# Forget gate and key of eight recurrent heads from one Tanh in place of two Sigmoids

## Chip, cores and metric

The kernel runs on one core of a Trainium2 chip. The metric is the device time of one launch in microseconds (us). The profile gives one execution of the same program. Its engines are PE (matmul; PEld is the weight load that overlaps it), DVE (vector), ACT (scalar, activation functions), POOL (GpSimd) and SP, which issues most transfers. Each engine works through its own queue in order and waits on semaphores for the others.

## What is computed

The reference is one inference step of a one-layer streaming encoder with two parallel branches: an mLSTM with 4 heads of width 512, and an HGRN2 recurrence with 8 heads of width 128. It runs on 512 new frames and on 32 frames of a running stream; the kernel treats them side by side as 544 columns. The change lies in the gates of the HGRN2 branch, where every weight has `q_h`, `f_h`, `i_h`, `g_h` as slices of one projection:

```
lb = cumsum(softmax(hgrn_lb, axis=0))[0]      # one number per channel
lfh = log(lb + (1 - lb) * sigmoid(f_h))       # log of the forget gate
kh  = (1 - lb) * sigmoid(-f_h)                # key
qh  = silu(q_h)
oh, S_new = _hgrn(qh, kh, i_h, lfh, S0)       # linear recurrence with decay exp(lfh)
oh = head_rmsnorm(oh) * silu(g_h)
```

## The kernel before

Channels lie on the 128 partitions and the 544 time steps along the row. The program has four stretches: the input norm with the first projections and the convolution; four mLSTM heads; eight recurrent heads; and the merge of the branches with the output projections.

All large products are single-precision products from two halves: each weight piece is split into a high part (a copy on ACT, lines 191 and 204) and a low part (a subtraction on DVE, lines 196 and 205), and three matmuls stand for one. Pairs of projection units are multiplied with seven block products in place of eight (`class Two`), which needs sums of weight pieces on DVE (line 533, tiles `ws`). Their results are taken out of PSUM by ACT (line 592, tiles `t`) and DVE (lines 599 and 601), and the last block of a unit calls what is to be done with the finished tile.

In the stretch of the recurrent heads (lines 1630 to 2000) three things are woven together. `Pump` walks through the block products of the projections still to be made, PE instruction by PE instruction, in units of half a block of 12 matmuls (line 575). `chain(h)` makes head h's matrix of attention and decay in seven levels (1, 2, 4, ... 64 columns): per level four or more matmuls of 128x128 (line 1815, tile `pl`), which read keys copied by ACT into one shared buffer (`keys`, line 1770, tile `kmos`) and the decayed query and key (tile `hkq`, a pair `kk` and `qq`); then DVE multiplies both by the decays of the level (line 1836), POOL multiplies the decays pairwise (line 1843), and DVE puts the products under masks (lines 1850 to 1852). `tail(h)` makes states and outputs of the head before. In this stretch the order on ACT, DVE and PE is that in which the code issues instructions; the constants `STEPS`, `PDGAP`, `PIECES`, `FDELAY`, `QDELAY` say after how many half blocks each piece is issued.

When the unit `f` of a head is finished, `forget(h, t)` is called with the pre-activation in `t` (tile `tf`; the last part comes by ACT, line 603). It issues on ACT: a Sigmoid of -t into `kk` at once (line 1642), and by `pump.defer` a Sigmoid of t in place after 2 half blocks (1643), the scaling of `kk` by `lc` = 1 - lb after 2 (1644), and lb + lc * t in place after 5 (1645). When unit `q` is finished, `query(h, t)` issues a Silu of t (line 1650, tile `hq`) and, after 2 half blocks, the product of query and forget gate on DVE (line 1653), which writes `qq`. The matmuls of level 1 (line 1815) read `qq` and the copied keys; the product with no decay (line 1790, tile `pd`) reads `kk` and `hq`. Between two heads' `forget` and `query` stand weight copies, PSUM copies and key copies of other work.

The instruction that loads a function table into ACT (ACT_TABLE_LOAD) isn't in the code; it is put ahead of an activation whose function isn't in the loaded table, and has that activation's line.

`hgrn_bounds` (line 1401) makes lb and lc once, from 128x8 numbers, in the first mLSTM head. The rest of that head's order on ACT and DVE is set by a scheduler, not by hand.

Of the kernel before, what the change touches and what calls it, by code (L numbers as in the profile page):

```python
# [9 lines left out]
F32 = mybir.dt.float32  # L10
# [3 lines left out]
AF = mybir.ActivationFunctionType  # L14
ALU = mybir.AluOpType

P = 128
# [4 lines left out]
T = NS + NP  # L22
# [5 lines left out]
HH = 8  # L28
# [17 lines left out]
VTGAP = ((2, 1, 1, 1, 1), (1, 1, 1, 1, 1), (1, 1, 1, 1, 1), (0, 2, 2, 1, 1))  # L46
GAPS = (20, 20, 20, 14)
APART = 10
FDELAY = (2, 2, 5)
QDELAY = 2  # L50
FACTORS = 0
HOLDS = (0, 1, 3)
# [31 lines left out]
def hybrid_step(ctx: ExitStack, tc: tile.TileContext, a, o):  # L84
    nc = tc.nc
    V, S, G, PE = nc.vector, nc.scalar, nc.gpsimd, nc.tensor

    cp = ctx.enter_context(tc.tile_pool(name="cp", bufs=1))
# [21 lines left out]
    def slot(name, dt=F32):  # L110
        return sp.tile([P, WP + P // 2], dt, tag="s", name=name)

    def eslot(name, dt=F32):

        return sp.tile([P, SLOT], dt, tag="e", name=name, bufs=NEVAC)

    def epair(name, dt=F32):

        return sp.tile([P, 2, SLOT], dt, tag="ee", name=name, bufs=2)

    def small(name, shape, dt=F32, bufs=2, tag=None):
        return tp.tile(shape, dt, tag=tag or name, name=name, bufs=bufs)
# [345 lines left out]
    def plain(t):  # L468

        return t, tuple(((t[:, b * TH : (b + 1) * TH], slice(0, TH)),) for b in range(2))  # L470
# [189 lines left out]
    def pair(what, f, unit, dest, then):  # L660

        return Two(
            [((what, f + i), unit + i, lambda f=f + i: dest(f), lambda t, f=f + i: then(f, t)) for i in range(2)]
        )
# [158 lines left out]
    def fill(h):  # L823


        def value(f, t):
            st8[h]["vt"][f] = t

        def gate(f, t):
            act = S.activation(t[:, :T], t[:, :T], AF.Silu)  # L830
            st8[h]["z"][f] = (t, act)

        def gate_one(f, acc):
            z = eslot(f"z{h}{f}")
            for b in range(2):
                act = S.activation(z[:, b * TH : (b + 1) * TH], acc[b][:, :TH], AF.Silu)
            st8[h]["z"][f] = (z, act)

        def inner_tile(f):
            ub = conv_tile((h + 1) * KH + f)  # L840
            return ub, conv_parts(ub)

        def inner(f, ub):
            st8[h + 1]["ub"][f] = ub
            if f == 0:
                conv(h + 1)

        st8[h]["z"] = [None] * KH
        todo = []
        if h:  # L850
            st8[h]["vt"] = [None] * KH
            todo += [pair("v", f, 16 + h * KH + f, lambda f: plain(eslot(f"vt{h}{f}")), value) for f in (0, 2)]
            todo += [pair("z", f, 32 + h * KH + f, lambda f: plain(eslot(f"z{h}{f}")), gate) for f in (0, 2)]
        else:
            todo += [One(("z", f), 32 + f, TH, lambda acc, f=f: gate_one(f, acc)) for f in range(KH)]
        if h + 1 < MH:
            st8[h + 1]["ub"] = [None] * KH
            todo += [pair("u", f, (h + 1) * KH + f, inner_tile, inner) for f in (0, 2)]
        else:
            todo.append(next(hgrn))  # L860
        return todo
# [534 lines left out]
        st8[h].clear()  # L1396
        return made[f"wbm{h}31"][1]

    lb, lc = cp.tile([P, HH], F32, name="lb"), cp.tile([P, HH], F32, name="lc")

    def hgrn_bounds(decayed, masked):

        l0, l1 = vec[:, V_LB : V_LB + HH], vec[:, V_LB + HH : V_LB + 2 * HH]
        lm, le = small("lbm", [P, HH], bufs=1), small("lbe", [P, 2, HH], bufs=1)
        with tc.issue_after(masked.ins):
            V.tensor_tensor(lm, l0, l1, ALU.max)
            V.tensor_tensor(le[:, 0, :], l0, lm, ALU.subtract)
            V.tensor_tensor(le[:, 1, :], l1, lm, ALU.subtract)
        with tc.issue_after(decayed.ins):
            S.activation(le, le, AF.Exp)  # L1410

        def rest():
            V.tensor_tensor(lm, le[:, 0, :], le[:, 1, :], ALU.add)
            V.reciprocal(lm, lm)
            V.tensor_tensor(lb, le[:, 0, :], lm, ALU.mult)
            V.tensor_tensor(lc, le[:, 1, :], lm, ALU.mult)

        return rest

# [25 lines left out]
    with tc.manual_schedule(engines={mybir.EngineType.Activation, mybir.EngineType.DVE, mybir.EngineType.PE}):  # L1445
# [15 lines left out]
        for k in range(KD):  # L1461
            t = xt[k]
# [133 lines left out]
        pump = Pump(fill(0))  # L1596
# [38 lines left out]
    def units():  # L1635


        def forget(h, t):
            lbc, lcc = lb[:, h : h + 1], lc[:, h : h + 1]
            kq = epair(f"hkq{h}")  # L1640
            kk = kq[:, 0]
            S.activation(kk[:, :T], t[:, :T], AF.Sigmoid, scale=-1.0)
            pump.defer(FDELAY[0], lambda: S.activation(t[:, :T], t[:, :T], AF.Sigmoid))
            pump.defer(FDELAY[1], lambda: S.mul(kk[:, :T], kk[:, :T], lcc))
            pump.defer(FDELAY[2], lambda: S.activation(t[:, :T], t[:, :T], AF.Identity, scale=lcc, bias=lbc))
            hs[h].update(tf=t, kk=kk, kq=kq)

        def query(h, t):
            qq = hs[h]["kq"][:, 1]
            S.activation(t[:, :T], t[:, :T], AF.Silu)  # L1650
            hs[h].update(q0=t, qq=qq)
            tf = hs[h]["tf"]
            pump.defer(QDELAY, lambda: V.tensor_tensor(qq[:, :T], t[:, :T], tf[:, :T], ALU.mult))  # L1653

        def turned(t):

            return t, (
                ((t[:, HB - 1 : HB - 1 - TH : -1], slice(0, TH)),),
                ((t[:, HB - 1 - TH :: -1], slice(0, HB - TH)), (t[:, HB:T], slice(HB - TH, TH))),
            )  # L1660

        def value(h, t):
            hs[h]["ii"] = t

        def gate(h, t):
            S.activation(t[:, :T], t[:, :T], AF.Silu)
            hs[h]["gg"] = t

        def merge_a(f, t):
            S.activation(t[:, :T], t[:, :T], AF.Sigmoid)  # L1670
            y = slot(f"ya{f}")[:, :T]
            nc.sync.dma_start(y, ya_d[f])
            pump.defer(2, lambda: V.tensor_tensor(y, y, t[:, :T], ALU.mult))
            yas[f] = y

        def merge_b(f, t):
            S.activation(t[:, :T], t[:, :T], AF.Sigmoid)
            gbs[f] = t

        for h in range(HH):  # L1680

            yield Two(
                [
                    (("q", h), 48 + h, lambda h=h: turned((slot if h else eslot)(f"hq{h}")), lambda t, h=h: query(h, t)),
                    (("f", h), 56 + h, lambda h=h: turned(eslot(f"tf{h}")), lambda t, h=h: forget(h, t)),
                ]
            )
            yield Two(
                [
                    (("g", h), 72 + h, lambda h=h: plain(eslot(f"hg{h}")), lambda t, h=h: gate(h, t)),  # L1690
                    (("i", h), 64 + h, lambda h=h: turned(eslot(f"hi{h}")), lambda t, h=h: value(h, t)),
                ]
            )
        for f in range(0, KD, 2):
            yield pair("ga", f, 80 + f, lambda f: plain(eslot(f"ga{f}")), merge_a)
            yield pair("gb", f, 88 + f, lambda f: plain(eslot(f"gb{f}")), merge_b)
# [3 lines left out]
    with tc.manual_schedule(engines={mybir.EngineType.PE}):  # L1700
        for h in range(MH):
# [16 lines left out]
            else:  # L1718
                pump = Pump(fill(h))
# [271 lines left out]
    with tc.manual_schedule(engines={mybir.EngineType.PE}):  # L1991
        pump = Pump(list(hgrn), staged=True)
# [17 lines left out]
    for k in range(2):  # L2010
        t = slot(f"p{k}")
# [46 lines left out]
    for k in range(KD // 2):  # L2058
        for f in (k, k + KD // 2):
            w = weight(a["w_brh"][f], f"wbh{f}", at=spread())  # L2060
            acc = dense(w, 0, P, P, obs, f"yb{f}")
            t = gbs[f]
# [13 lines left out]
    def output(f, t):  # L2076
        h1s[f] = psplit(t[:, :T], "h1", f)

    with tc.manual_schedule(engines={mybir.EngineType.PE}):
        pump = Pump(  # L2080
            [
                Onto([(("o", f), f, lambda f=f: plain(h1[f]), lambda t, f=f: output(f, t)) for f in (k, k + KD // 2)], ys, yf)
                for k in range(KD // 2)
            ],
            src=a["w_out"],
        )
# [167 lines left out]
```

## Time and profile before

| what | value |
|---|---|
| time, median of 3 runs | 1104.61 us (1103.64 to 1105.09) |
| profiled execution, its own time | 1106.07 us |
| its span, first to last instruction | 1104.3 us |
| recurrent heads on PE, after the last mLSTM matmuls | about 613 to 865 us of the span |

Of the profile, several views are used. The page gives busy time by engine. The windows view gives busy time of each engine in stretches of the span. The view of waits tells which line of an engine waited for whom, in total us, number of times and longest us. The timeline lists instructions by start time and duration; in brackets is the idle time of the engine just before, with what ended it. A matmul's duration includes its way through the array, so matmuls that follow each other without a stall overlap: the distance between two starts, not the duration, tells what a matmul costs.

### The profile page before, as it was taken

How to read it: one execution, taken by the hardware profiler on the slowest of the kernel's cores; microseconds unless marked ns; L12 is line 12 of the kernel's file. 1: busy time of each engine (PE TensorE's matmuls, PEld its weight loads, DVE VectorE, ACT ScalarE, POOL GpSimd, SP SyncE). 2: the span in 40 equal slices, each digit the busy share in tenths (PEclk: the TensorE clock that was granted, in tenths of full speed). 3: DMA queues.
4: the chain of work that ended last, by engine and by line, in shares of the span. 5: the costliest groups of instructions: out<-in, count | busy, mean ns of one | idle time of the engine just before them, and what ended most of it. 6: DMA issues, size and time to landing. Idle time of an engine off the chain costs nothing.

```text
span 1104.3 us, 23737 instructions
## 1 busy us (share of the span) xinstructions
PE 1089.9 (99%) x8765; PEld 1077.4 (98%) x8765; DVE 920.8 (83%) x1989; ACT 712.2 (64%) x1571; POOL 173.0 (16%) x417
## 2 busy tenths in 40 slices
PE   9999999999999999999999999999999999999998
PEld 9999999999999999999999999999999999999998
DVE  6986999679798596986898688999999888789885
ACT  6686656755666455664566478887777767445762
POOL 2122024111010130101100123322332100000000
PEclk9999999999999999999999999999999999999999
DMA  6223225634365344464556222122221353343743
GB/s 224 78 96 107 83 86 174 146 100 127 105 206 160 81 147 144 126 225 92 157 159 218 95 78 84 56 80 80 85 75 62 111 178 116 116 124 116 260 146 121
DMA packets 104781, 138.67 MB, mean 126 GB/s; under 512 B 35765, under 2 KB 43573, under 8 KB 104665
## 3 DMA queue, kind: packets, MB, share of 16 engines
q1 hardware_dynamic: 104496, 137.10, 40.0%
q8 instruction: 69, 1.13, 0.4%
q14 instruction: 48, 0.39, 0.1%
q10 hardware_dynamic: 168, 0.06, 0.0%
HBM read 110.96 MB, written 26.16 MB: 124 GB/s over the span
## 4 chain that ended last, share of the span: by engine, by line
PE 59%; DVE 12%; ACT 7%; issue 2%; DMA 0%; POOL 0%; DVEq 0%; ACTq 0%; POOLq 0%
PE d L575 26%; PE ya L229 6%; PE pg L2099 4%; PE yb L229 4%; PE C L1112 3%; PE q L229 3%; DVE ws L533 2%; PE k L229 2%; PE sc L1054 2%; DVE hkq L1836 2%; PE nm L1313 2%; PE ple L229 1%; DVE at L1852 1%; DVE ws L508 1%; ACT shared L1947 1%
## 5 line engine op out<-in xcount | busy, mean ns | idle before, releaser
L592 ACT COPY t<-d 128x272 f32<-128x272 f32 x126 | 47.5, 377 | 20.8 <-PE d L575 20.7
L1770 ACT COPY kmos<-hkq 128x256 f32<-128x256 f32 x56 | 23.9, 427 | 38.0 <-DVE hkq L1836 34.7
L1836 DVE TENSOR_TENSOR hkq<-hkq,hq 128x288 f32<-128x288 f32 (+1 forms) x96 | 41.4, 438 | 1.5
L1815 PE MATMUL pl<-hkq,kmos 128*128 128x128 f32 x224 | 35.5, 279 | 3.3 <-DVE hkq L1653 1.9
L801 DVE SCALAR_TENSOR_TENSOR cv<-ub,vec,cv 128x547 f32<-128x547 f32 x48 | 37.1, 782 | 0.4
L1815 PEld LDWEIGHTS pl<-hkq,kmos 128*128 128x128 f32 x224 | 30.0, 188 | 4.9 <-ACT kmos L1770 1.5
L1112 PE MATMUL C<-vh,kwl 128*128 128x256 f32 x96 | 27.0, 281 | 0.0
L1112 PE MATMUL C<-vl,kwh 128*128 128x256 f32 x96 | 26.9, 280 | 0.0
L1112 PE MATMUL C<-vh,kwh 128*128 128x256 f32 x96 | 26.8, 279 | 0.0
L1392 DVE TENSOR_TENSOR y<-ya,y 128x272 f32<-128x272 f32 x48 | 18.8, 434 | 8.0 <-PE ya L229 7.8
L1852 DVE COPY_PREDICATED at<-lmask,pl 128x256 f32<-128x256 uint8 x56 | 25.0, 446 | 0.0
L1313 PE MATMUL nm<-vh,sh 128*128 128x256 f32 x80 | 22.8, 285 | 1.0 <-ACT Co L1124 0.6
L1324 ACT COPY y<-nm 128x516 f32<-128x516 f32 x16 | 9.4, 588 | 21.5 <-PE nm L1313 21.5
L1313 PE MATMUL nm<-vl,sh 128*128 128x256 f32 x80 | 22.6, 282 | 0.0
L963 POOL COPY vsm<-vt 128x96 f32<-128x96 f32 x16 | 12.8, 809 | 62.2 <-DVE vt L599 43.9
L1313 PE MATMUL nm<-vh,sl 128*128 128x256 f32 x80 | 22.5, 281 | 0.0
L1068 ACT CAST sh<-dm 128x512 fp32r<-128x512 f32 (+3 forms) x16 | 7.4, 459 | 22.8 <-DVE dm L1062 22.8
L1054 PE MATMUL sc<-q,kh 128*128 128x512 f32 (+3 forms) x80 | 18.6, 321 | 0.0
L1243 DVE SCALAR_TENSOR_TENSOR c<-c,wi,Cs 128x256 f32<-128x256 f32 (+1 forms) x32 | 14.9, 471 | 4.1 <-PE Cs L1241 4.0
L1112 PEld LDWEIGHTS C<-vh,kwh 128*128 128x128 f32 x96 | 18.1, 189 | 0.0
L1112 PEld LDWEIGHTS C<-vl,kwh 128*128 128x128 f32 x96 | 18.1, 188 | 0.0
L1112 PEld LDWEIGHTS C<-vh,kwl 128*128 128x128 f32 x96 | 18.0, 188 | 0.0
(5767 smaller groups left out, 5164.6 us busy)
## 6 DMA issues: line engine op xcount, KB each, us to landing
ya_d<-y SPq DMA_DIRECT2D x32, 272.0 KB, 3.1
y<-ya_d SPq DMA_DIRECT2D x24, 272.0 KB, 3.1
c<-in_C SPq DMA_DIRECT2D x16, 258.0 KB, 3.6
out_Cs<-c SPq DMA_DIRECT2D x16, 258.0 KB, 2.6
out_Cp<-Co SPq DMA_DIRECT2D x15, 258.0 KB, 2.5
k_d<-kf SPq DMA_DIRECT2D x48, 68.0 KB, 2.0
x<-in_xT SPq DMA_DIRECT2D x8, 272.5 KB, 4.6
ya<-ya_d SPq DMA_DIRECT2D x8, 272.0 KB, 4.7
```

The costliest lines, as they stand in the source:

```text
L229: PE.matmul(both[b][:m, :TH], part(w, off + k * step, m, x), xx[:, half(b)], start=(k == 0 and j == 0), stop=(k == n - 1 and j == 2),)
L575: PE.matmul(ps, ww[:, c], xx, start=(start and k == 0 and j == 0), stop=end, skip_group_check=not start,)
L592: S.copy(t, ps)
L801: last = V.scalar_tensor_tensor(cv[:, :547], ub[:, j : j + 547], vcol(V_CW + 4 * ft + j), cv[:, :547], ALU.mult, ALU.add)
L1054: PE.matmul(pn[:, 0, :n], ks[f][x][:, j * P : (j + 1) * P], qs[f][y][:, NS + j * P : T], start=(f == 0 and i == 0), stop=(f == KH - 1 and ...
L1112: PE.matmul(pn[g], kw[b][x][:, f * P : (f + 1) * P], vv[b][y][:, VS[g]], start=(b == 0 and j == 0), stop=(b == NB - 1 and j == 2),)
L1313: PE.matmul(pn[:, g, VP[g] : VP[g] + VN[g]], st[j][x][:, (i - j) * P : (i - j + 1) * P], vv[j][y][:, VS[g]], start=(j == 0 and q == 0), st ...
L1770: S.copy(km.rearrange("p (n j c) -> p n j c", j=2, c=c), view(kk, HB, ((2 * c, NA // (2 * c)), (c - HB, 2), (1, c))),)
L1815: PE.matmul(pn[:, b * P : (b + 1) * P].rearrange("p (n j c) -> p j n c", j=2, c=c), km[:, b * P : (b + 1) * P], view(qq, b * P, ((HB + c, ...
L1836: V.tensor_tensor(x, x, t, ALU.mult)
L1852: V.copy_predicated(blocks2(at[:, :NA]), twice(lmask[:, li, :P]), blocks2(pn[:, :NA]))
L2099: PE.matmul(ps, part(w, k * P, P, x), xx[:, c], start=(k == 0 and j == 0), stop=(k == KD - 1 and j == 2))
```

## The change

`forget` makes the key from th = tanh(-t/2): since sigmoid(-t) = (1 + th)/2, the key (1 - lb) * sigmoid(-t) is half * th + half with half = (1 - lb)/2. The forget gate lb + (1 - lb) * sigmoid(t) is lb + (1 - lb) minus the key. So there is one Tanh in place, one Identity with scale and bias from memory into `kk`, and one Identity with scale -1 and bias from memory back into `t`. `FDELAY` becomes (2, 4): the key after 2 half blocks, the forget gate after 4.

```diff
-FDELAY = (2, 2, 5)
+FDELAY = (2, 4)
...
-            V.tensor_tensor(lb, le[:, 0, :], lm, ALU.mult)
-            V.tensor_tensor(lc, le[:, 1, :], lm, ALU.mult)
+            V.tensor_tensor(lsum, le[:, 0, :], lm, ALU.mult)
+            V.tensor_tensor(le[:, 1, :], le[:, 1, :], lm, ALU.mult)
+            V.tensor_tensor(lsum, lsum, le[:, 1, :], ALU.add)
+            V.tensor_scalar(lhalf, le[:, 1, :], 0.5, None, ALU.mult)
...
-            lbc, lcc = lb[:, h : h + 1], lc[:, h : h + 1]
+            whole, part_ = lsum[:, h : h + 1], lhalf[:, h : h + 1]
             kq = epair(f"hkq{h}")
             kk = kq[:, 0]
-            S.activation(kk[:, :T], t[:, :T], AF.Sigmoid, scale=-1.0)
-            pump.defer(FDELAY[0], lambda: S.activation(t[:, :T], t[:, :T], AF.Sigmoid))
-            pump.defer(FDELAY[1], lambda: S.mul(kk[:, :T], kk[:, :T], lcc))
-            pump.defer(FDELAY[2], lambda: S.activation(t[:, :T], t[:, :T], AF.Identity, scale=lcc, bias=lbc))
+            S.activation(t[:, :T], t[:, :T], AF.Tanh, scale=-0.5)
+            pump.defer(FDELAY[0], lambda: S.activation(kk[:, :T], t[:, :T], AF.Identity, scale=part_, bias=part_))
+            pump.defer(FDELAY[1], lambda: S.activation(t[:, :T], kk[:, :T], AF.Identity, scale=-1.0, bias=whole))
             hs[h].update(tf=t, kk=kk, kq=kq)
```

The built programs show what this moves. ACT around the gates of head 3 stands like this before; `wa1152h` and `ws175h` are high parts of weight pieces, `wa2275h` as well, `t` is a PSUM copy.

```order
L1642 ACT_TABLE_LOAD
L1642 ACTIVATE hkq_10352<-tf_10019 128x544
L191 CAST wa1152h<-wi52r_10170 128x512
L592 COPY t_10373<-d_10257 128x272
L1770 COPY kmos<-hkq_9900 128x256
L1643 ACTIVATE tf_10019<-tf_10019 128x544
L1644 ACTIVATE hkq_10352<-hkq_10352,lc 128x544
L191 CAST ws175h<-ws_10174 128x512
L1650 ACT_TABLE_LOAD
L1650 ACTIVATE hq_10018<-hq_10018 128x544
L191 CAST wa2275h<-wi67r_10008 128x512
L1645 ACTIVATE tf_10019<-tf_10019,lb,lc 128x544
```

And like this with the change (the line numbers are those of the changed kernel):

```order
L1644 ACTIVATE tf_10018<-tf_10018 128x544
L191 CAST wa1152h<-wi52r_10169 128x512
L592 COPY t_10372<-d_10256 128x272
L1771 COPY kmos<-hkq_9900 128x256
L1645 ACTIVATE hkq_10351<-tf_10018,lhalf 128x544
L191 CAST ws175h<-ws_10173 128x512
L1646 ACTIVATE tf_10018<-hkq_10351,lsum 128x544
L1651 ACTIVATE hq_10017<-hq_10017 128x544
L191 CAST wa2275h<-wi67r_10007 128x512
```

Both table loads and one activation are gone, and the write of the forget gate stands ahead of the Silu. The other heads from 2 on look the same; head 0 had two more table loads, at lines 1643 and 1666. Of 30 table loads in the program 12 are left, none of them in the heads. DVE, POOL, PE and SP keep their order from head 1 to the end of the program.

At the hand-over from the last mLSTM head to head 0, DVE stood like this before; `y<-ya` takes a product of the mLSTM branch out of PSUM.

```order
L205 TENSOR_TENSOR wbm320l<-wbm32r_8920,wbm320h 128x512
L1392 TENSOR_TENSOR y_8784<-ya_8786,y_8784 128x272
L1392 TENSOR_TENSOR y_8784<-ya_8787,y_8784 128x272
L1392 TENSOR_TENSOR y_8815<-ya_8817,y_8815 128x272
L1392 TENSOR_TENSOR y_8815<-ya_8818,y_8815 128x272
L1653 TENSOR_TENSOR hkq_8720<-hq_8511,tf_8512 128x544
L205 TENSOR_TENSOR wbm321l<-wbm32r_8922,wbm321h 128x512
```

With the change:

```order
L205 TENSOR_TENSOR wbm320l<-wbm32r_8921,wbm320h 128x512
L205 TENSOR_TENSOR wbm321l<-wbm32r_8923,wbm321h 128x512
L1654 TENSOR_TENSOR hkq_8722<-hq_8513,tf_8514 128x544
L1392 TENSOR_TENSOR y_8785<-ya_8787,y_8785 128x272
L1392 TENSOR_TENSOR y_8785<-ya_8788,y_8785 128x272
L205 TENSOR_TENSOR wbm330l<-wbm33r_8995,wbm330h 128x512
L1392 TENSOR_TENSOR y_8816<-ya_8818,y_8816 128x272
L1392 TENSOR_TENSOR y_8816<-ya_8819,y_8816 128x272
```

The product of head 0's query and forget gate has moved ahead of the first two pairs of PSUM reads. Lastly, in the first mLSTM head, where `hgrn_bounds` has its two more instructions on DVE, the scheduler has set some instructions in another order. On ACT, in which `y<-nm` takes a product out of PSUM and `xfh` is the high part of a sum, it was:

```order
L1124 COPY Co_2009<-C_1984 128x516
L405 CAST xfh_1831<-xu_1833 128x544
L1324 COPY y_2039<-nm_2032 128x516
L409 ACTIVATE xfh_1831<-xv_1835 128x272
L1324 COPY y_2058<-nm_2045 128x516
```

With the change:

```order
L1124 COPY Co_2011<-C_1986 128x516
L1324 COPY y_2041<-nm_2034 128x516
L405 CAST xfh_1833<-xu_1835 128x544
L1324 COPY y_2060<-nm_2047 128x516
L409 ACTIVATE xfh_1833<-xv_1837 128x272
```

The first read of PSUM has moved ahead of a copy that waits for DVE. On DVE some twenty rows of the same head are in another order, with nothing but the two instructions added.

More of the change, by code (lines that the diff above doesn't have):

```diff
@@ L1397, in stage_br @@
         return made[f"wbm{h}31"][1]
-    lb, lc = cp.tile([P, HH], F32, name="lb"), cp.tile([P, HH], F32, name="lc")
+    lsum, lhalf = cp.tile([P, HH], F32, name="lsum"), cp.tile([P, HH], F32, name="lhalf")
     def hgrn_bounds(decayed, masked):
```

## The prediction

> **What bounds the kernel now.** I read the page first.
>
> ```profile
> span 1104.3 us, 23737 instructions
> PE 1089.9 (99%) x8765; PEld 1077.4 (98%) x8765; DVE 920.8 (83%) x1989; ACT 712.2 (64%) x1571; POOL 173.0 (16%) x417
> ```
>
> PE is busy nearly all the time, ACT is not. The change takes work from ACT alone, so it can pay only where PE stands still for something that ACT made late. PE does the same instructions in the same order afterwards; the most there is to win is its standstill in the recurrent heads. The windows view gives it (columns: window, length, then busy us of PE, PEld, DVE, ACT, POOL with counts, granted clock, transfers).
>
> ```profile
> 585.00:620.00 35.00, 35.00 (x286) 35.00 (x285) 24.18 (x50) 18.20 (x30) 1.40 (x3) 1.00 0.62 207
> 620.00:865.00 245.00, 240.74 (x1960) 237.40 (x1959) 222.16 (x497) 193.63 (x480) 71.64 (x160) 1.00 0.25 78
> ```
>
> In the hand-over before 620 us PE has no gap at all. In the heads, to 865 us, it is idle for 245.00 - 240.74 = 4.3 us, its weight loads for 245.00 - 237.40 = 7.6 us. The first undercounts, since a matmul's duration covers the start of a stall behind it; the second overcounts, since loads are shorter than the matmuls beside them. The truth should lie between. Next the waits of PE in the heads:
>
> ```profile
> PE pl L1815 <- DVE hkq L1653: 1.9, 5, 0.4
> PE pl L1815 <- ACT kmos L1770: 1.0, 1, 1.0
> PE d L575 <- DVE hg L599: 0.7, 1, 0.7
> PE pl L1815 <- ACT ws255h L191: 0.4, 1, 0.4
> ```
>
> Five waits of 0.4 us for the product of query and forget gate (line 1653). The last row is a sixth of the kind: `pl` doesn't read `ws255h`, which merely ended last there. These six are heads 2 to 7; the other two stand in head 1. So there are two things to explain: a small stall once per head, and two larger ones.
>
> **The change part by part.** *ACT's own time.* The groups by line:
>
> ```profile
> L1642 ACT ACT_TABLE_LOAD x8 | 10.3, 1283 | 0.1
> L1645 ACT ACTIVATE tf<-tf,lb,lc 128x544 f32<-128x544 f32 x8 | 6.7, 836 | 0.0
> L1644 ACT ACTIVATE hkq<-hkq,lc 128x544 f32<-128x544 f32 x8 | 5.9, 737 | 0.0
> L1642 ACT ACTIVATE hkq<-tf 128x544 f32<-128x544 f32 x8 | 5.3, 659 | 0.1
> ```
>
> A head now has two table loads of 1.28 us, two Sigmoids of 0.66 (the second is at 705.89 below), one scaling of 0.74 and one with two memory operands of 0.84: 5.46 us. Afterwards: a Tanh, not in the trace, which I take at the Sigmoid's 0.66 (same size and operands; 0.84 at most, the dearest row here); the key with two memory operands, 0.84; the gate with one, 0.74: 2.24 us. That is 3.2 us less per head, 25.8 us for eight heads and 2.6 us for head 0's two further loads: 28 us of ACT. The program's order has no table load left in the heads, so that the loads might stay is not a case.
>
> *Heads 2 to 7.* Head 3 in the timeline, ACT, DVE and PE:
>
> ```profile
> 702.94 1.28 ACT L1642 ACT_TABLE_LOAD   x1
> 704.23 0.66 ACT L1642 ACTIVATE hkq<-tf 128x544 f32<-128x544 f32 x1
> 704.80 0.60 ACT L191 CAST wa1152h<-wi52r 128x512 fp32r<-128x512 f32 x1
> 705.30 0.38 ACT L592 COPY t<-d 128x272 f32<-128x272 f32 x1
> 705.58 0.41 ACT L1770 COPY kmos<-hkq 128x256 f32<-128x256 f32 x1
> 705.89 0.66 ACT L1643 ACTIVATE tf<-tf 128x544 f32<-128x544 f32 x1
> 706.45 0.74 ACT L1644 ACTIVATE hkq<-hkq,lc 128x544 f32<-128x544 f32 x1
> 707.09 0.61 ACT L191 CAST ws175h<-ws 128x512 fp32r<-128x512 f32 x1
> ```
>
> ```profile
> 704.25 0.88 DVE L1836 TENSOR_TENSOR hkq<-hkq,hq 128x256 f32<-128x256 f32 x2
> 706.04 0.50 DVE L599 TENSOR_TENSOR hq<-d,t 128x16 f32<-128x16 f32 x2
> 707.73 0.69 DVE L196 TENSOR_TENSOR ws175l<-ws,ws175h 128x512 fp32r<-128x512 f32 x1 [1.19 <-ACT ws175h L191]
> 711.16 0.70 DVE L1653 TENSOR_TENSOR hkq<-hq,tf 128x544 f32<-128x544 f32 x1
> ```
>
> ```profile
> 711.22 0.29 PE L575 MATMUL d<-xfl,ws175h 128*128 128x272 f32 x1
> 711.34 0.28 PE L575 MATMUL d<-xfh,ws175l 128*128 128x272 f32 x1
> 712.01 0.71 PE L1815 MATMUL pl<-hkq,kmos 128*128 128x128 f32 x4 [0.38 <-DVE hkq L1653]
> ```
>
> Read it from the end. `pl` starts 0.67 us after the matmul before it, where 0.12 is usual: a stall of 0.55 us. It waited for the product on DVE, which ended at 711.86. DVE was not waiting for the forget gate there; it came late out of its own queue, which ran without a gap from 707.73 on. That run began late because DVE had stood 1.19 us before `ws175l`, waiting for ACT's copy `ws175h`. And that copy stood behind a table load, two Sigmoids and the key's scaling. So the table load costs PE 0.55 us by way of a weight piece that has nothing to do with it.
>
> Afterwards: Tanh 702.94 to 703.5, `wa1152h` to 704.1, the PSUM copy to 704.4. Then the key copy `kmos` must wait for DVE's second product, which ends at 705.13; this swallows most of what was gained. It ends about 705.45, the key about 706.1, and `ws175h` starts at 706.05 or so in place of 707.09. The 1.85 us taken out ahead of it (1.29 from 702.94 to 704.23, and 0.56 from 705.89 to 706.45) become about 1.0 us. DVE's `ws175l` starts near 706.7; ahead of it DVE is done at 706.54. The run to the product then ends near 710.8, and PE, without the stall, wants it at 711.46. Half a microsecond to spare: the whole 0.55 us goes. The gate and the Silu have changed places; the Silu loses a load of 1.28 ahead of it and gets the gate's 0.74, so what reads it, POOL's first copy and `pd`, isn't later either. What is late next is nothing on DVE by the same account, as its queue moves by 1.0 us and PE only by 0.55. Six heads give 6 x 0.55 = **3.3 us**; bounds 0 (another wait takes the place of `ws175h`) and 3.9 (0.1 more per head).
>
> Here a rule of the Trainium skill can be weighed. DVE and PE rows give 0.55 us a head, between the 4.3 us and 7.6 us above. "Perfetto Trace Analysis", section "Identifying the Most-Contended Engine", says that matmul busy time is no measure of what is left, and that the busy share of the weight loads is; by that the heads hold 7.6 us, and if the change freed them all its gain would be that. I keep the distances between starts, and make the other a rival below.
>
> *Head 1.* Two other waits.
>
> ```profile
> 639.61 0.40 ACT L603 ACTIVATE tf<-d 128x272 f32<-128x272 f32 x1
> 641.88 0.39 ACT L1770 COPY kmos<-hkq 128x256 f32<-128x256 f32 x1
> 639.86 0.88 DVE L1836 TENSOR_TENSOR hkq<-hkq,hq 128x256 f32<-128x256 f32 x2
> 641.00 0.28 PE L575 MATMUL d<-xh,ws449l 128*128 128x272 f32 x1
> 642.32 0.71 PE L1815 MATMUL pl<-hkq,kmos 128*128 128x128 f32 x4 [1.03 <-ACT kmos L1770]
> ```
>
> The key copy of the level stands right behind the table load and the first Sigmoid. With a Tanh alone ahead of it (640.0 to 640.6) it starts when DVE is done, at 639.86 + 0.88 = 640.74, and ends at 641.13; PE follows at about 641.2 in place of 642.32. Gain **1.1 us** of the 1.20 (1.32 less the pitch).
>
> ```profile
> 648.03 0.73 DVE L1653 TENSOR_TENSOR hkq<-hq,tf 128x544 f32<-128x544 f32 x1 [1.05 <-ACT tf L1645]
> 649.16 0.39 PE L575 MATMUL d<-xfh,ws173h 128*128 128x272 f32 x1 [0.72 <-DVE hg L599]
> ```
>
> Here the forget gate itself is late: DVE's product waits 1.05 us for it, the PSUM read `hg` stands behind the product, and PE waits for the bank. ACT comes about 1.15 us earlier out of the key copy, saves the second Sigmoid and the second load (1.84) and has the gate ahead of a weight copy: over 2 us earlier, against PE's 1.1. The stall goes: gain **0.7 us**, by its mark.
>
> *Hand-over to head 0.* PE has no gap there to win. DVE's product now stands ahead of the first four reads of `ya`. Head 0 has three loads ahead of the gate (3.85 us) and a Sigmoid (0.66) that go, and a weight copy (0.6) that comes; the product starts near 592.6 in place of 596.55, and the reads come 1.3 us later than now:
>
> ```profile
> 592.03 0.79 DVE L1392 TENSOR_TENSOR y<-ya,y 128x272 f32<-128x272 f32 x2 [0.18 <-PE ya L229]
> 596.55 0.73 DVE L1653 TENSOR_TENSOR hkq<-hq,tf 128x544 f32<-128x544 f32 x1 [0.78 <-ACT tf L1645]
> 594.91 0.41 PE L229 MATMUL ya<-hm12h,wbm310h 128*128 128x272 f32 x2
> ```
>
> A third `ya` unit starts on PE at 594.91 and needs the banks of the first. The reads end near 594.1, in time: I cost this at 0, with a cover of 0.8 us (the bound is in the last rival). SP's weight loads and stores change places there by one or two; the transfers have 585 to 620 us with no PE wait to show for them.
>
> *First mLSTM head.* Two more DVE instructions on 128x8 numbers, which hide in DVE's queue as long as no PSUM read behind them is late, and another order.
>
> ```profile
> 134.81 0.65 ACT L405 CAST xfh<-xu 128x544 fp32r<-128x544 f32 x1 [1.06 <-DVE xu L402]
> 136.00 0.38 PE L1313 MATMUL nm<-vh,sh 128*128 128x256 f32 x1 [0.49 <-ACT y L1324]
> ```
>
> PE stands 0.49 us for a PSUM copy that sits behind `xfh`; that copy now comes first, and the stall should go. Against it, DVE's order is shuffled. I take 0.3 us of gain, bounds -1.0 (a loss of twice PE's mark) and +0.5.
>
> **The sum.** 3.3 + 1.1 + 0.7 + 0.3 = 5.4 us. Against the profiled execution's own 1106.07 us (a span of 1104.3 and 1.8 around it) that is 1100.7; the runs' median of 1104.61 lies 1.5 lower, which gives **1099.2 us**, 0.5% faster. By about 0.2%, or 2.2 us, a measurement of this kernel can tell a change from none.
>
> **The rivals.** *All of the weight loads' idle time goes.* The heads would run with no gap at all: 1104.6 - 7.6 = 1097.0. Against it: most of this idle time is matmuls that hide a shorter load, which no change on ACT alters. This is what the rule of the Trainium skill named above would give. Chance 0.06.
>
> *DVE takes ACT's place in heads 2 to 7.* DVE is busy 222 of the 245 us, and the key copies on ACT wait for it far more than it waits for ACT:
>
> ```profile
> ACT kmos L1770 <- DVE hkq L1836: 32.3, 29, 2.6
> ```
>
> If `ws175l` finds another wait (the sum `ws`, a ring buffer that PE hasn't left), the stall of 0.55 us stays and only head 1 and the first mLSTM head's 0.3 count: 2.1 us, up to 3.8 if half of the heads gain; about 1101.7. Chance 0.16.
>
> *ACT's time was hidden all along.* The copies ahead of each stall wait for DVE as before and nothing moves: 1104.3. Head 1's key copy, with no DVE wait marked, speaks against. Chance 0.12.
>
> *Slower.* The place is the hand-over. If the forget gate of head 0 were no earlier than now, the product would hold DVE's queue until 597.3 and four reads of `ya` behind it; PE would wait from 594.91 to about 598.1, 3.2 us, and a gate that late means that the heads' ACT queue had not become shorter either: 1107.8. It decides when the product starts after 594.1. ACT's rows speak against it, since the loads ahead of the gate are gone. Chance 0.06.
>
> **The numbers.** Forecast 0.60, rivals 0.06, 0.16, 0.12, 0.06. Faster by over 0.2% (under 1102.4): 0.60 + 0.06 + most of 0.16 = 0.79; within 0.2%: 0.15; slower: 0.06. The forecast's own bounds are 1098.4 (3.9 and 0.5 for heads and first mLSTM head) and 1100.5 (a loss of 1.0 there). The range leaves out the last two rivals and ends at 1103.0; at the low end 1097.4 takes in the runs' scatter of 1 us.
>
> **What would show it.** No table load in 589 to 860 us; the distance from the last `d` matmul to `pl` after the product near 0.15 us in heads 2 to 7; DVE's idle mark before `ws175l` down from 1.19 to about 0.2; in head 1 the waits for `kmos` and `hg` gone; PE idle in the heads down from 4.3 to under 1 us, and the last head's end 5 us earlier. Wrong if the mark before `ws175l` falls but `pl` still waits for line 1653's successor (DVE bound), if a new PE wait for `ya` reads appears near 595 us, or if the time before 585 us moves by over 1 us.

## The result and the profile with the change

The changed kernel takes 1096.66 us (median of 6 runs, 1095.73 to 1097.29) where the kernel before takes 1104.69 beside it (6 runs). The ratio is 0.9927, with a 95% interval of 0.9914 to 0.994: 8.0 us faster, where 5.4 were forecast. The time lies 0.7 us below the low end of the range. The profiled execution took 1097.29 us; against the profiled execution of before that is 8.8 us, since that one lay 1.4 us above its median and this one 0.6.

The page first, span and busy times.

```profile
span 1095.6 us, 23704 instructions
PE 1086.1 (99%) x8765; PEld 1075.6 (98%) x8765; DVE 920.7 (84%) x1991; ACT 684.8 (63%) x1545; POOL 180.9 (17%) x417
```

ACT has lost 27.4 us of work (28 worked out), and DVE's busy time has not moved. Of the 12 table loads left, one does fall into the stretch of the heads: it stands at 849.87 us, ahead of the Sigmoid of the merge (line 1671), as it stood at 858.44 before. So the sign "no table load in 589 to 860 us" isn't met to the letter, but the gates of the heads have none. The windows view of the hand-over and the heads shows where PE gained.

```profile
585.00:620.00 35.00, 35.00 (x287) 35.00 (x286) 23.66 (x48) 13.20 (x24) 2.79 (x5) 1.00 0.61 203
620.00:865.00 245.00, 244.80 (x2025) 243.81 (x2025) 229.25 (x510) 178.49 (x478) 70.93 (x158) 1.00 0.26 81
```

The hand-over is as full as before. In the heads PE's idle time has gone from 4.3 to 0.2 us, that of the weight loads from 7.6 to 1.2. The groups of ACT by line show the prices of the three activations.

```profile
L1645 ACT ACTIVATE hkq<-tf,lhalf 128x544 f32<-128x544 f32 x8 | 6.7, 842 | 0.0
L1646 ACT ACTIVATE tf<-hkq,lsum 128x544 f32<-128x544 f32 x8 | 6.0, 746 | 0.0
L1644 ACT ACTIVATE tf<-tf 128x544 f32<-128x544 f32 x8 | 5.3, 658 | 0.2
```

Tanh 0.66, key 0.84, gate 0.75: as taken. Head 3 in the timeline, ACT first.

```profile
698.52 0.66 ACT L1644 ACTIVATE tf<-tf 128x544 f32<-128x544 f32 x1
699.08 0.60 ACT L191 CAST wa1152h<-wi52r 128x512 fp32r<-128x512 f32 x1
699.59 0.38 ACT L592 COPY t<-d 128x272 f32<-128x272 f32 x1
700.78 0.41 ACT L1771 COPY kmos<-hkq 128x256 f32<-128x256 f32 x1 [0.81 <-DVE hkq L1837]
701.10 0.84 ACT L1645 ACTIVATE hkq<-tf,lhalf 128x544 f32<-128x544 f32 x1
701.84 0.60 ACT L191 CAST ws175h<-ws 128x512 fp32r<-128x512 f32 x1
```

As forecast, the key copy `kmos` now waits for DVE (0.81 us) and swallows part of what was taken out. From the table load to `ws175h` it was 707.09 - 702.94 = 4.15 us; from the Tanh in its place it is 701.84 - 698.52 = 3.32. DVE and PE of the same head:

```profile
702.48 0.69 DVE L196 TENSOR_TENSOR ws175l<-ws,ws175h 128x512 fp32r<-128x512 f32 x1 [0.43 <-ACT ws175h L191]
705.89 0.72 DVE L1654 TENSOR_TENSOR hkq<-hq,tf 128x544 f32<-128x544 f32 x1
```

```profile
705.78 1.05 PE L1791 MATMUL pd<-hq,hkq 128*128 128x128 f32 x8
707.29 0.29 PE L575 MATMUL d<-xfh,ws175l 128*128 128x272 f32 x1
707.42 0.63 PE L1816 MATMUL pl<-hkq,kmos 128*128 128x128 f32 x4
```

`pd` takes 1.05 us; this will matter below. DVE's idle mark is 0.43 in place of 1.19, the product ends at 706.61, and `pl` follows the matmul ahead of it after 0.13 us, where it was 0.67. So the chain that the prediction followed is there. But the heads gained more than this stall. The first `pl` behind the product, in heads 2 and 7, in the timeline of the kernel before:

```profile
680.91 0.36 PE L1815 MATMUL pl<-hkq,kmos 128*128 128x128 f32 x1 [0.39 <-DVE hkq L1653]
836.41 0.35 PE L1815 MATMUL pl<-hkq,kmos 128*128 128x128 f32 x1 [0.38 <-DVE hkq L1653]
```

And the same two with the change:

```profile
677.30 0.28 PE L1816 MATMUL pl<-hkq,kmos 128*128 128x128 f32 x1
828.02 0.28 PE L1816 MATMUL pl<-hkq,kmos 128*128 128x128 f32 x1
```

Five heads lie between them: 155.50 / 5 = 31.10 us a head before, 150.72 / 5 = 30.14 now. PE does the same matmuls, so a head had lost 0.96 us, not 0.55. Matched instruction by instruction, the start times of PE's matmuls in the two traces differ by 0.7 us when head 1 begins, by 2.7 at its end (the key copy 1.04, the forget gate 0.97), and by 8.4 at the end of head 7: 5.7 us for heads 2 to 7.

Where the other 0.4 us of a head were, the timeline of before shows in two groups of eight matmuls: `su`, which reads ACT's copy of the turned key, and `pd`, which reads the Silu's result.

```profile
690.11 0.28 PE L575 MATMUL d<-xh,wa1251l 128*128 128x272 f32 x1
690.29 1.16 PE L1912 MATMUL su<-hi,hkq 128*128 128x128 f32 x8
...
709.57 0.29 PE L575 MATMUL d<-xh,wa1152l 128*128 128x272 f32 x1
709.72 1.16 PE L1790 MATMUL pd<-hq,hkq 128*128 128x128 f32 x8
```

ACT ahead of them, in the same trace:

```profile
689.67 0.57 ACT L1904 COPY hkq<-ht 128x512 f32<-128x512 f32 x1
...
709.01 0.66 ACT L1650 ACTIVATE hq<-hq 128x544 f32<-128x544 f32 x1
```

The copy ends at 690.24 and `su` starts at 690.29; the Silu ends at 709.67 and `pd` starts at 709.72. Each starts 0.05 us behind ACT, and 0.18 and 0.15 behind the matmul before it, where 0.13 is usual. Neither has an idle mark, because the matmul ahead still runs for 0.28 us by the trace. But eight matmuls take 1.16 us after such a wait, and with the change 1.05:

```profile
686.35 0.29 PE L575 MATMUL d<-xh,wa1251l 128*128 128x272 f32 x1
686.48 1.05 PE L1913 MATMUL su<-hi,hkq 128*128 128x128 f32 x8
```

So a wait of 0.05 us costs some 0.16: itself, and 0.1 more inside the group. The weight loads of the same two groups, before and with the change, tell where the tenth goes:

```profile
690.29 0.97 PEld L1912 LDWEIGHTS su<-hi,hkq 128*128 128x128 f32 x8
...
686.35 0.98 PEld L1913 LDWEIGHTS su<-hi,hkq 128*128 128x128 f32 x8
```

With the change the first load starts 0.13 us ahead of its matmul (686.48), as the loads before it do. Before, it starts with its matmul (690.29), and the second load stands 0.11 us behind the first, with the second matmul another 0.11 behind its load. A wait takes away the loads' lead over the matmuls, and the lead is worth 0.1 us. The same tenth stands behind the marked wait at `pl` (0.71 us for four matmuls at 712.01, 0.63 now). Per head that makes 0.55 + 0.08 at `pl`, about 0.16 at `su`, about 0.1 at `pd` and 0.04 in the matmuls that follow `pl`: 0.93.

### The profile page after: what moved, and what is told of

It reads as the page before. It is cut to its first block, busy times and chain, and to the rows that moved or that the text cites. A ratio compares the mean times of both kernels' runs of the same rounds, so it can differ in the third digit from the quotient of the medians.

```text
span 1095.6 us, 23704 instructions
## 1 busy us (share of the span) xinstructions
PE 1086.1 (99%) x8765; PEld 1075.6 (98%) x8765; DVE 920.7 (84%) x1991; ACT 684.8 (63%) x1545; POOL 180.9 (17%) x417
## 4 chain that ended last, share of the span: by engine, by line
PE 76%; DVE 3%; issue 1%; DMA 0%; ACT 0%; POOL 0%; ACTq 0%; DVEq 0%; POOLq 0%
PE d L575 39%; PE ya L229 6%; PE pg L2100 4%; PE yb L229 4%; PE C L1112 3%; PE q L229 3%; PE pl L1816 2%; PE k L229 2%; PE sc L1054 2%; PE nm L1313 2%; PE ple L229 1%; DVE ws L508 1%; PE su L1913 1%; PE ho L1936 1%; PE ht L1896 1%
## 5 line engine op out<-in xcount | busy, mean ns | idle before, releaser
L963 POOL COPY vsm<-vt 128x96 f32<-128x96 f32 x16 | 16.4, 1035 | 58.6 <-DVE vt L599 43.9
L793 POOL COPY uo<-ub 128x3 f32<-128x3 f32 x16 | 17.8, 1112 | 30.6 <-DVE ub L601 23.5
```

## The experiments

The theory that the experiments test: in heads 2 to 7 PE was held up by what ACT made late, directly (`su`, `pd`) and by way of DVE's queue (`pl`); with the change PE's own 30.14 us a head sets the pace, and ACT has some slack. The chief rival: time simply follows the amount of ACT's work, so that the 27 us removed buy 8 wherever they stand. Times are medians.

| kernel | us | before beside it | ratio, 95% interval |
|---|---|---|---|
| with the change | 1096.66 | 1104.69 | 0.9927 (0.9914 to 0.994) |
| only the loads gone | 1100.28 | 1104.71 | 0.9957 (0.9945 to 0.997) |
| change, loads put back | 1102.14 | 1104.71 | 0.9975 (0.9964 to 0.9986) |
| only the bounds | 1104.32 | 1104.71 | 1.0002 (0.9993 to 1.0011) |
| change, pass ahead of `kmos` | 1096.90 | 1104.71 | 0.9928 (0.9915 to 0.994) |
| change, pass behind `kmos` | 1101.91 | 1104.22 | 0.9979 (0.997 to 0.9988) |
| change, key's copy late | 1100.99 | 1104.22 | 0.9974 (0.9964 to 0.9984) |
| change, gate last | 1095.88 | 1104.22 | 0.9925 (0.9912 to 0.9937) |
| before, order alone | 1103.29 | 1104.22 | 0.999 (0.9981 to 0.9999) |

What the traces of these kernels say of a head stands in a second table. "Period" is the mean distance from head to head between the first `pl` behind the product. Of the three groups of matmuls it gives two distances between starts in us, usual for heads 3 to 6: from the matmul ahead to the first of the group, and from the first to the second.

| kernel | period | `pl` | `su` | `pd` |
|---|---|---|---|---|
| before | 31.10 | 0.67, 0.19 | 0.18, 0.21 | 0.13 to 0.15, 0.16 to 0.21 |
| with the change | 30.14 | 0.13, 0.12 | 0.13, 0.11 | 0.13, 0.11 |
| only the loads gone | 30.70 (30.78 from head 3 on) | 0.40 to 0.47, 0.19 | 0.18, 0.21 | 0.13, 0.11 |
| change, loads put back | 30.86 | 0.13, 0.12 | 0.18, 0.21 | 0.47, 0.21 |
| only the bounds | 31.09 | 0.67, 0.19 | 0.19, 0.21 | 0.13 to 0.14, 0.16 to 0.21 |
| change, pass ahead of `kmos` | 30.26 | 0.13, 0.12 | 0.12 to 0.20, 0.21 | 0.13, 0.11 |
| change, pass behind `kmos` | 31.17 | 0.78 to 0.88, 0.19 | 0.19, 0.21 | 0.13, 0.11 |
| change, key's copy late | 30.79 | 0.13, 0.12 | 0.70, 0.21 | 0.13, 0.11 |
| change, gate last | 30.17 | 0.13, 0.12 | 0.12 to 0.16, 0.11 to 0.21 | 0.13, 0.11 |
| before, order alone | 30.94 | 0.48, 0.19 | 0.19, 0.21 | 0.15, 0.21 |

In each row the excess over 0.13 and 0.11 (0.12 at `pl`), added up, comes within 0.15 us of the excess of the period over 30.14: before it is 0.54 + 0.07 + 0.05 + 0.10 + 0.01 + 0.08 = 0.85 against 0.96.

### Only the table loads gone

```diff
-            S.activation(kk[:, :T], t[:, :T], AF.Sigmoid, scale=-1.0)
-            pump.defer(FDELAY[0], lambda: S.activation(t[:, :T], t[:, :T], AF.Sigmoid))
+            S.activation(kk[:, :T], t[:, :T], AF.Tanh, scale=-1.0)
+            pump.defer(FDELAY[0], lambda: S.activation(t[:, :T], t[:, :T], AF.Tanh))
```

> The kernel before with Tanh in place of both Sigmoids, nothing else: the table loads go, all four passes and their order stay. It leaves out the sigmoids, so gate and key have other values. Theory (the loads made ACT late at three places per head: the weight copy, the Silu, the key's PSUM copy): the key copy's wait for DVE swallows part, the weight copy comes 0.45 us earlier, pl keeps 0.1 to 0.2 us of its stall, the small stalls at pd and su go: 6 x 0.8 + 1.8 in head 1 = 6.6 us, 1098.1 (1097.5 to 1099). Rival 1 (the saved pass is what counts): under 2 us of gain, 1103. Rival 2 (all of the gain is the loads): 1097.4, as much as the change less its first mLSTM head.

Measured: 1100.28, a gain of 4.4 us, between the theory and the first rival, and outside the theory's range. Head 1 got all of its 2.0 us, head 2 some 1.3 once, and each later head only about 0.3. Head 3 in its timeline, ACT and then DVE:

```profile
701.22 0.41 ACT L1770 COPY kmos<-hkq 128x256 f32<-128x256 f32 x1 [0.82 <-DVE hkq L1836]
701.53 0.66 ACT L1643 ACTIVATE tf<-tf 128x544 f32<-128x544 f32 x1
702.09 0.73 ACT L1644 ACTIVATE hkq<-hkq,lc 128x544 f32<-128x544 f32 x1
702.73 0.60 ACT L191 CAST ws175h<-ws 128x512 fp32r<-128x512 f32 x1
```

```profile
703.37 0.69 DVE L196 TENSOR_TENSOR ws175l<-ws,ws175h 128x512 fp32r<-128x512 f32 x1 [0.89 <-ACT ws175h L191]
```

The load of 1.28 us stood ahead of `kmos`. With it gone, `kmos` waits 0.82 us for DVE, and the two passes behind `kmos` still keep `ws175h`: DVE's mark falls by 0.3 only, from 1.19 to 0.89, and so does the period. `pl` and `su` still wait; `pd` doesn't. What comes off ahead of a wait for another engine is mostly eaten by that wait. The loads alone are little over half of the gain.

### The change with its table loads put back

```diff
+            S.activation(kk[:1, :2], t[:1, :2], AF.Sigmoid)
             S.activation(t[:, :T], t[:, :T], AF.Tanh, scale=-0.5)
```

> The changed kernel with a Sigmoid of 1x2 elements ahead of each Tanh, so that two table loads per head return; the saved pass stays saved. Theory: the weight copy is 0.35 us earlier than before, but the Silu, now behind gate and load, 0.2 us later: heads 2 to 7 win 0.1 us each, head 1 0.8, the first mLSTM head 0.7: 1102.6 (1101.5 to 1104). Rival (fewer and shorter passes are what counts, not loads): 1098 or less.

Measured: 1102.14, as the theory had it, but not by the stall that I meant. The waits of PE in its heads:

```profile
PE pl L1817 <- ACT kmos L1772: 1.3, 1, 1.3
PE pd L1792 <- ACT hq L1652: 1.1, 6, 0.2
```

The first row is head 1's, as before the change. In the later heads the wait at `pl` for DVE's product is gone and stays gone. In its place `pd` waits in six heads for the Silu, which stands behind the second load, and starts 0.47 us after the matmul ahead of it. By the traces head 1 wins 0.8 us, as expected, and each later head 0.24 (31.10 less 30.86) where 0.1 was expected. The loads cost 5.5 us here and 4.4 in the kernel before, at another place. What a late ACT costs is set by the next thing that PE reads from it.

### Only the two instructions in `hgrn_bounds`

```diff
+    lsum, lhalf = (cp.tile([P, HH], F32, name=n) for n in ("lsum", "lhalf"))
...
+            V.tensor_tensor(lsum, lb, lc, ALU.add)
+            V.tensor_scalar(lhalf, lc, 0.5, None, ALU.mult)
```

> The kernel before with the two small DVE instructions in hgrn_bounds and nothing else; the order of the first mLSTM head on ACT and DVE becomes that of the changed kernel, the gates stay. Theory: 0.7 us faster (1104.0), PE 0.5 to 1.0 us earlier at 585 us, heads as before. Rival (the shift before the heads is scatter of the execution): 1104.7, no shift.

Measured: a ratio of 1.0002, with an interval of -0.8 to +1.2 us. The stall of 0.49 us at 136.00 us has no row in its view of waits, nor in that of the changed kernel, but 0.2 us come back at 138.5 us. Its profiled execution (1104.23 us) is 2.3 us ahead of before's at 585 us, that of the change only 0.7. Single executions scatter there by over 2 us: the traces of six kernels that have the changed kernel's program up to the heads reach one and the same matmul at 578.9 to 581.3 us. So this part wins at most 0.8 us, and these two expectations, 0.7 us apart, are not told apart.

### An extra pass ahead of `kmos`, and one behind it

The first makes the Tanh twice, once into `kk`, which stands ahead of `kmos`. The second makes the key's Identity twice, behind `kmos` in heads 1 to 7 (in head 0 behind the Silu, with the product behind the first pair of reads of `ya`).

```diff
+            S.activation(kk[:, :T], t[:, :T], AF.Tanh, scale=-0.5)
             S.activation(t[:, :T], t[:, :T], AF.Tanh, scale=-0.5)
```

```diff
-            pump.defer(FDELAY[0], lambda: S.activation(kk[:, :T], t[:, :T], AF.Identity, scale=part_, bias=part_))
+            pump.defer(FDELAY[0], lambda: [S.activation(kk[:, :T], t[:, :T], AF.Identity, scale=part_, bias=part_) for _ in range(2)])
```

> The changed kernel with the Tanh made twice (first into the key's buffer, which is overwritten later): 0.56 us more on ACT ahead of the key copy in every head. Theory: the key copy waits 0.8 us for DVE there, so the pass is hidden and nothing behind it moves: 1096.7 (up to 1097.3). Rival (time follows ACT's total in the heads, 28 us of which gave 7.3): 8 x 0.66 = 5.3 us more give 1.4: 1098.1.

> The changed kernel with the key's Identity made twice into the same tile: one pass over 544 numbers more per head, 0.74 us from start to start, behind the key copy kmos and ahead of the weight copy ws175h. It is a pass of the same width as that of the extra-pass kernel, which stood ahead of kmos and cost nothing. Theory: here kmos's wait for DVE can't hide it; ws175h and DVE's queue behind it come 0.74 later, and the product of query and forget gate, which was ready 0.5 to 0.8 us ahead of pl, is late; from head to head the loop of ACT and DVE gets longer than PE's 30.16 us, by about 0.6 to 0.9 us. 6 heads: 1100.9 us (1099 to 1102). Rival 1 (time follows the sum of ACT's work; 28 us of it bought 8.0, so 5.9 cost 1.7): 1098.4. Rival 2 (hidden as the other pass was): 1096.8.

Measured: by the medians the first costs 0.2 us, less than their scatter. Its trace shows that it isn't free: from the first `pl` of head 0 to the last of head 7 it takes 0.9 us longer than the change alone, half of it at head 1's `kmos` and 0.12 a head where `su` waits again. The second takes 1101.91 beside 1104.22, which is 2.3 us faster than before where the change is 8.0 faster: it costs 5.7 us, and 5.7 by the traces too. Passes of the same width, ACT time within 0.3 us a head, and 0.9 against 5.7 us: the place decides, and the rival that time follows ACT's work is out. Head 3 of the second kernel, ACT, DVE, PE:

```profile
701.06 0.41 ACT L1771 COPY kmos<-hkq 128x256 f32<-128x256 f32 x1 [0.81 <-DVE hkq L1837]
701.37 1.72 ACT L1645 ACTIVATE hkq<-tf,lhalf 128x544 f32<-128x544 f32 x2
702.99 0.61 ACT L191 CAST ws175h<-ws 128x512 fp32r<-128x512 f32 x1
```

```profile
703.63 0.69 DVE L196 TENSOR_TENSOR ws175l<-ws,ws175h 128x512 fp32r<-128x512 f32 x1 [1.32 <-ACT ws175h L191]
```

```profile
707.03 0.29 PE L575 MATMUL d<-xfh,ws175l 128*128 128x272 f32 x1
707.91 0.71 PE L1816 MATMUL pl<-hkq,kmos 128*128 128x128 f32 x4 [0.59 <-DVE hkq L1654]
```

It is the head of before again, with no table load in it: DVE's mark ahead of `ws175l` (1.32), `pl` late (0.88 from start to start), four matmuls at 0.71. The short waits come back with it: set against the changed kernel, each head from 3 on loses 0.66 to 0.75 at `pl`, 0.07 at the next `pl`, 0.06 at the first matmul of `su` and 0.10 at the second. So the waits at `su` belong to the same lateness of ACT. The forecast for it, 1100.9, was 1.0 too low, by these terms.

### The key's copy late

```diff
-            S.copy(dst, pt)
+            for _ in range(1 if src is ii else 3):
+                S.copy(dst, pt)
```

> The changed kernel with ACT's copy of the turned key out of PSUM (line 1905, the one for kk) made three times, so that it ends some 1.04 us later in each of the eight heads (0.57 us each, 0.52 from start to start). Theory: before the change this copy ended 0.05 us ahead of the first su matmul and held PE up a little without a row in the view of waits; after it, it ends about 0.5 us ahead of su's weight load (685.82 against 686.35). So su waits here by 0.5 us, and loses about 0.1 more at the second su matmul: 0.6 us in each of 8 heads, 4.8 us: 1101.5 us (1100 to 1103), with a wait of PE's su for this copy in the view. Rival (the short waits at su have another cause, and ACT's copy has 1 us or more of slack): 1096.7.

Measured: 1100.99 beside 1104.22, 4.8 us more than the change costs alone: the theory's figure. The waits of PE and the same `su` in the timeline:

```profile
PE su L1914 <- ACT hkq L1906: 3.7, 7, 1.1
```

```profile
685.29 0.29 PE L575 MATMUL d<-xh,wa1251l 128*128 128x272 f32 x1
686.06 1.16 PE L1914 MATMUL su<-hi,hkq 128*128 128x128 f32 x8 [0.48 <-ACT hkq L1906]
```

The three copies end at 686.01, `su` starts 0.05 later, and eight matmuls take 1.16 us as before the change. The first is 0.64 us late and the group 0.11 longer: PE's view of waits shows 0.48 of these 0.75. The same view of the weight loads shows more, 0.70 here and 5.2 us in place of 3.7 in all:

```profile
686.06 0.97 PEld L1914 LDWEIGHTS su<-hi,hkq 128*128 128x128 f32 x8 [0.70 <-ACT hkq L1906]
PEld su L1914 <- ACT hkq L1906: 5.2, 7, 1.4
```

The 0.11 is the same after an unmarked wait of 0.05 us (before) and after one of 0.64. At `pl` and `pd` nothing moved: this copy makes `su` late and nothing else, so `su` is a cost of its own beside `pl`.

### The forget gate last, and the order alone

```diff
-FDELAY = (2, 4)
+FDELAY = (2, 5)
```

> The changed kernel with FDELAY (2, 5) in place of (2, 4): the forget gate's write stands behind the Silu and the weight copy wa2275h again, as in the kernel before; DVE, POOL, PE and SP keep their order. Theory: the gate then ends about 1.2 us later, near 704.4 in head 3, and its product does not start before 705.9, so nothing moves: 1096.7 us (1096.2 to 1097.4). Rival (the new place of the gate is part of the gain, because DVE's product waits for it): 0.3 to 0.5 us per head, 1098.5 to 1100.

Measured: a ratio of 0.9925 where the change has 0.9927, and the same period. The gate's place ahead of the Silu, in the changed kernel, is worth nothing that can be measured; it has slack. In the kernel before, order was tried alone:

```diff
-FDELAY = (2, 2, 5)
+FDELAY = (3, 3, 5)
```

> The kernel before with FDELAY (3, 3, 5): the second Sigmoid and the key's scaling stand behind the weight copy ws175h in heads 1 to 7, which so comes 1.3 us earlier; all of ACT's work is kept, loads too, and no other engine's order changes. Theory: DVE's run begins earlier and its idle mark ahead of ws175l goes, but the forget gate ends when it did, about 711.0 in head 3, and the product of query and forget gate, which began at 711.16, now waits for it: about 0.15 us per head is won, 1103.6 us (1102.8 to 1104.4). Rival (the stall at pl hangs on ws175h's place alone): 0.55 to 0.9 us for each of 6 heads, 1099 to 1101.4.

Measured: 1103.29 beside 1104.22, the ratio just under 1: 0.9 us, and 0.18 us at each `pl`, as the theory said. Head 3, DVE in this kernel:

```profile
705.57 0.69 DVE L196 TENSOR_TENSOR ws175l<-ws,ws175h 128x512 fp32r<-128x512 f32 x1
...
710.00 0.73 DVE L1653 TENSOR_TENSOR hkq<-hq,tf 128x544 f32<-128x544 f32 x1 [0.91 <-ACT tf L1645]
```

The mark ahead of `ws175l` is gone altogether, and it has moved: DVE stands 0.91 us ahead of the product, for the forget gate, which ACT can't make sooner with its loads and passes in the way. In the kernel before, the gate stood here on ACT:

```profile
710.08 0.84 ACT L1645 ACTIVATE tf<-tf,lb,lc 128x544 f32<-128x544 f32 x1
```

It ended at 710.92, 0.24 us ahead of the product's start at 711.16. So the prediction's remark that DVE "was not waiting for the forget gate there" was true by 0.24 us: the gate was the next late thing behind `ws175h`. To reorder is not enough; the work had to go.

## Why the prediction was right in kind and short in size

- *What bounds the kernel* was right: PE, by its standstill in the heads, behind a weight piece that ACT copied late. Of 245 us PE's idle time fell from 4.3 to 0.2.
- *ACT's own time*: 28 us worked out, 27.4 measured. The Tanh's price was right.
- *Six heads give 6 x 0.55* is the step that failed, in its size. The stall of 0.55 us went as described, with 0.8 us to spare (706.61 against 707.42) where half a microsecond was expected. But a head gained 0.94, and the six 5.7 us; the bound of 3.9 was too tight as well. I had measured the largest gap of a head and taken the rest of PE's starts as fixed. The rest held the tenth behind each wait and two waits, at `su` and `pd`, that PE's view of waits doesn't mark. The view of the weight loads' waits in the kernel before would have hinted at them: it has 0.6 us in place of 0.4 at each `pl`, and `pd` waiting for the Silu, though once only and for 0.2 us. The two traces show them by their group lengths, 1.16 against 1.05, and the late copy (`su`), the pass behind `kmos` (`pl`, with `su`) and the loads put back (`pd`, with `su`) brought them back.
- *Between 4.3 us and 7.6 us.* The forecast had the right brackets in hand; 3.3 + 1.8 = 5.1 was taken near the lower one, and 2.0 + 5.7 = 7.7 was true, at the upper one. I held that the loads' idle time was mostly matmuls that hide a shorter load. That was wrong: with the change the loads are idle for 1.2 us of 245.
- By the rule of the Trainium skill's "Perfetto Trace Analysis", section "Identifying the Most-Contended Engine", the busy share of the weight loads tells what is left, and not that of the matmuls. The trace agrees here: 7.6 us by the rule, 7.7 measured. That the two meet so closely is in part luck. Over the same matmuls (620.27 to 861.84 us before, 619.59 to 853.29 now) the loads' idle time falls from 7.6 to 1.1 us, which is 6.5 of the 7.9 us won there; the other 1.4 are busy time of the loads that has become shorter. The rival that I gave 0.06, that all of the weight loads' idle time goes, came nearest with its 1097.0.
- *Head 1* was forecast at 1.1 + 0.7 and gave 1.04 + 0.97. At the gate I had counted the mark alone, 0.7, which is again less than the stall.
- *Hand-over*, 0: right, as the product started at 591.39 by the trace, ahead of the 594.1 from which it would have cost.
- *First mLSTM head*, 0.3: not settled, a gain of 0.8 us at most.
- *DVE takes ACT's place* did not come about: DVE still waits 0.43 us ahead of `ws175l`, and `pl` waits for nothing. Part of it, another wait in the place of the one removed, is what happens when only the order is changed, or only the loads.

In sum: 0.3 + 0 + 1.8 + 3.3 = 5.4 forecast, and by the profiled executions 0.7 ahead of the heads, 2.0 in head 1 and 5.7 in the six others, 8.4 of the 8.8. The medians make it 8.0.

## What to carry to other kernels

Don't price a repeated stage by its largest marked wait: take the period of the stage from one repeat to the next, set it against what the bound engine's instructions need back to back, and count the whole difference as what can be won. Compare the lengths of equal groups of matmuls (1.16 against 1.05 us) to find waits that are too short for a mark, and look at the waits of the weight loads beside those of the matmuls. Work ahead of a wait for another engine is worth little (here 0.9 us in all), the same work behind that wait all of its time (5.7 us). Before an order is changed, look at what will be late next.

## What the runs showed of the hardware

A group of small matmuls that has waited for its operand takes up to 0.1 us longer than one that hasn't: the second of `su` or `pd` starts 0.21 us after the first in place of 0.11, of `pl` 0.19 in place of 0.12. It is the same after a wait of 0.05 us and after one of 0.64. With a short wait this costs more than the wait itself, and PE's view of waits shows neither. What is lost is the lead of the weight loads, so a group can lose it without a late first matmul: with the loads put back, another `pl` group in heads 3 to 7 starts its first load 0.01 to 0.03 us ahead in place of 0.12, its first matmul in time, and its second 0.19 to 0.21 us after the first in place of 0.11. And Tanh and Silu follow each other in every head without a table load, while a Sigmoid of two numbers ahead of each Tanh brings back two of 1.28 us a head.
